# One channel of the z projection moved into the modulation stream

## The chip, the core and the metric

The kernel runs on one NeuronCore of a Trainium2 chip, whose engines work side by side, each through its own queue in order: TensorE (PE in the rows; PEld is its weight loads), VectorE (DVE), ScalarE (ACT), GpSimd (POOL) and SyncE (SP), which here issues most DMAs. The metric is the device time of one execution in microseconds, lower is better.

## The reference, cut to what matters

The block is an RG-LRU and a differential attention side by side, then a mixture of experts, over 1024 tokens of width 1024. The part that the change touches:

```python
mod = jnp.dot(jax.nn.silu(c), w_mod[l]) + b_mod[l]
shift1, scale1, gate1, shift2, scale2, gate2 = jnp.split(mod[:, None, :], 6, axis=-1)
h = rms_norm(x, g_norm1[l]) * (1.0 + scale1) + shift1
proj = jnp.dot(h, w_in[l])
x_lru, z_lru, q, k, v = jnp.split(proj, SPLITS, axis=-1)   # 512 columns each
xc = lax.conv_general_dilated(x_lru, conv_w[l], ...) + conv_b[l]
h_fwd = rg_lru(xc, ..., False)
h_bwd = rg_lru(xc, ..., True)
y_lru = (h_fwd + h_bwd) * jax.nn.gelu(z_lru)
```

After it come the attention on q, k and v, the output product with w_out, the router, and 16 experts.

## The kernel before, in words

h is kept transposed: 8 row blocks of 128 model rows by 1024 tokens. Each product with w_in is done in three parts for exactness: a weight tile is split into a high part (a ScalarE copy) and the low rest (a subtraction on VectorE or GpSimd), h likewise into hh and hl, and wh·hh, wl·hh and wh·hl are summed in PSUM. For one channel block (128 columns of w_in) that is 8 row blocks x 3 parts x 2 halves of 512 tokens = 48 matmuls.

**The modulation stream** (L377 to L440) makes h block by block, in an order written out by hand for TensorE, VectorE and ScalarE (manual_schedule). For row block k: m_load (L281) brings the block's columns of w_mod for shift and scale, m_mm (L293) multiplies part of them by silu(c) on TensorE into tile mp, m_sum (L300) adds the rest on VectorE into acc (L304, L310), m_red (L314) sums acc over partitions on TensorE into the small tile pm, m_col (L319) makes the block's scale and shift columns, h_make (L325) makes hh on ScalarE and hl on GpSimd or VectorE. At once x_mm (L340) multiplies the block with w_in's columns 0 to 255, that is two channel blocks of x_lru (px[0] and px[1]), the wl·hh and wh·hh parts in iteration k and the wh·hl part one iteration later. Iteration k of the loop at L412 works on modulation block k + 2 and on products of block k.

**PSUM** has four tiles of two banks in this phase, two under the tag "pj" and two under "pg". In the stream px[0] and px[1] hold one of each; mp uses the other "pj" and pm the other "pg".

**Behind the stream** the order is found by a planner that lists instructions by priority and modelled time, engine by engine: do_x (L452) is the convolution on VectorE, do_lru (L495) a channel block's gates (products pg on TensorE, tanh and exp on ScalarE tg, tt) and its two scans on VectorE, proj_qk (L576) the dense q and k products (pjq, pjk) with their norms (rq, nq) and a flip to channel order (pbq, pbk; then hq/hk on ScalarE and lq/lk on VectorE), mod_rest (L618) the remaining four modulation rows, 32 loads wr of 512 KB each added up on VectorE into macc, mod_out (L625) their sum over partitions (mq), do_z (L636) one channel block of z (proj_ch, pjz) and fin_lru (L535), which multiplies gelu(z) with the scans' sum. do_z for channels 0 and 1 stands at L657 and L661, behind the k products; their weights are wz0 (L653).

**Buffers that tie the loads to the work:** raw weights go through 5 buffers (rawA), split ones through 6 (strm), the scans through 10 (lru), w0's split parts, macc and the results y_lru share 4 (ylp).

Of the kernel before, what the change touches and what calls it, by code (L numbers as in the profile page):

```python
# [8 lines left out]
F32 = mybir.dt.float32  # L9
F32R = mybir.dt.float32r  # L10
# [8 lines left out]
P = 128  # L19
# [4 lines left out]
NCT = 4  # L24
# [38 lines left out]
KV = (7,)  # L63
KH = (0, 1, 2, 7)
KB = (0, 1, 2, 7)
CAP = 128
RPAD = 56
EPS = 1e-6
# [14 lines left out]
def tile_block(ctx: ExitStack, tc, x, cols, w_mod, b_mod, w_in, wa, wx, lam_qk, relT, w_out, g2, w_router,  # L83
# [5 lines left out]
    def act(out, in_, func=AF.Copy, **kw):  # L89
        return A.activation(out=out, in_=in_, func=func, **kw)  # L90
# [42 lines left out]
    def raw_tile(name, shape):  # L133
        return rawA.tile(shape, F32, tag="raw", bufs=NRA, name=name)
# [4 lines left out]
    def split(src, hi, lo, eng=None):  # L139
        act(hi, src)  # L140
        return (eng or V).tensor_tensor(out=lo, in0=src, in1=hi.bitcast(F32), op=ALU.subtract)  # L141

    def load_half(c0, kk, eng):
        r = raw_tile(f"wi{c0}_{kk}", [P, 4, 256])
        SY.dma_start(out=r, in_=w_in[kk * 512:(kk + 1) * 512, c0:c0 + 256].rearrange("(k p) c -> p k c", p=P))
        hi = strm.tile([P, 4, 256], F32R, tag="s", bufs=NSP, name=f"wi{c0}_{kk}h")
        lo = strm.tile([P, 4, 256], F32R, tag="s", bufs=NSP, name=f"wi{c0}_{kk}l")
        split(r, hi, lo, eng)
        return hi, lo

    def load_in(c0, eng):
        return [load_half(c0, kk, eng) for kk in range(2)]

    phb = ExitStack()
    psb = phb.enter_context(tc.tile_pool(name="psb", bufs=1, space=PSUM, reuse_waits="tile"))
# [125 lines left out]
    def m_load(k):  # L281
        for rh in range(2):
            w = raw_tile(f"wm{k}_{rh}", [P, 4, 2, P]) if rh else v_tile(f"wm{k}_{rh}", [P, 4, 2, P])
            for g in range(2):
                c0 = g * 1024 + k * P
                with tc.issue_after(lds[-1].ins):
                    lds.append(SY.dma_start(out=w[:, :, g, :],
                                            in_=w_mod[rh * 512:(rh + 1) * 512, c0:c0 + P].rearrange("(r p) c -> p r c", p=P)))
            wm[k, rh] = w

    mps, pms = {}, {}

    def m_mm(k):  # L293
        if RP[k]:
            mps[k] = psb.tile([P, 2, P], F32, tag="pj", bufs=2, name=f"mp{k}")
        for r in range(RP[k]):
            g = 32 * (r % 4)
            mm(mps[k][g:g + 32], scz[:, r, :], wm[k, r // 4][:, r % 4], r < 4, r + 4 >= RP[k])
# [13 lines left out]
            V.tensor_tensor(out=part[0], in0=part[0], in1=part[1], op=ALU.add)  # L312

    def m_red(k):  # L314
        pms[k] = psb.tile([P, 2], F32, tag="pg", bufs=2, name=f"pm{k}")
        for g in range(2):
            mm(pms[k][:, g:g + 1], accs[k][:, g, :], ones32[:, 0:1], True, True)

# [21 lines left out]
    def x_mm(k, lo, ms=(0, 1)):  # L340
        for m in ms:
            wh, wl = (w[:, k % 4, m * P:(m + 1) * P] for w in ws0[k // 4])
            for lt, h_ in ((wh, hl[k]),) if lo else ((wh, hh[k]), (wl, hh[k])):
                for n in range(2):
                    mm(px[m][:, n * 512:(n + 1) * 512], lt, h_[:, n * 512:(n + 1) * 512],
                       k == 0 and lt is wh and not lo, k == KT - 1 and lo)

    w0r, wq0 = [], []

    def w0_load(kk):  # L350
# [5 lines left out]
    def w0_split(kk, part):  # L356
        if part == 0:
            ws0.append([ylp.tile([P, 4, 256], F32R, tag="y", bufs=NCT, name=f"w0{c}_{kk}") for c in "hl"])
            act(ws0[kk][0], w0r[kk])
        else:  # L360
            hi, lo = ws0[kk]
            V.tensor_tensor(out=lo, in0=w0r[kk], in1=hi.bitcast(F32), op=ALU.subtract)
# [6 lines left out]
    w0_load(0)  # L369
    for k in range(1, 4):  # L370
        m_load(k)
        if k == KM:
            w0_load(1)
    with tc.issue_after(lds[-1].ins):
# [2 lines left out]
    with tc.manual_schedule(engines={mybir.EngineType.PE, mybir.EngineType.DVE, mybir.EngineType.Activation}):  # L377
        c_silu()
        tables_a()
        act(rst[:, 0:1], epsc, AF.Sqrt)  # L380
        for t in range(NT + 1):
            if t < NT:
                x_stat(t)
            if 1 <= t <= NT:
                if t == NT:
                    m_mm(0)
                    m_sum(0)
                x_flip(t - 1)
                if t == NT:
                    m_red(0)  # L390
            if 2 <= t <= NT:
                x_evac(t - 2)
        w0_split(0, 0)
        m_col(0)
        x_evac(NT - 1, (0,))
        m_mm(1)
        warm(WU1)
        w0_split(0, 1)
        m_sum(1)
        h_make(0)  # L400
        m_red(1)
        m_col(1)
        x_evac(NT - 1, (1,))
        h_make(1)
        x_mm(0, False)
        m_mm(2)
        m_sum(2)
        x_mm(1, False, (0,))
        m_red(2)
        m_col(2)  # L410
        h_make(2)
        for k in range(1, KT + 1):  # L412
            if k + 3 < KT:
                m_load(k + 3)
            if k + 2 < KT:
                m_mm(k + 2)
                m_sum(k + 2)
            if k == KS:
                w0_split(1, 1)
            if k == 1:  # L420
                x_mm(0, True)
            if k == KLT:
                lam_table()
            if k < KT:
                x_mm(k, False, (0, 1) if k > 1 else (1,))
            if 1 < k < KT:
                x_mm(k - 1, True)
            if k + 2 < KT:
                m_red(k + 2)
                m_col(k + 2)  # L430
                i_act, i_pv = h_make(k + 2)
                if k + 2 < KT - 1:
                    i_pool = i_pv
                else:
                    i_dve = i_pv
            if k == KS0:
                w0_split(1, 0)
            if k + 2 in (KW, KW + 1):
                wq0.append(load_half(1024, k + 2 - KW, V))
        x_mm(KT - 1, True)  # L440
    sm1_.close()


# [51 lines left out]
    def do_lru(ct):  # L495
        xc = xc_[ct]
        xh = lt_(f"xch{ct}", None, F32R)
        xl = lt_(f"xcl{ct}", None, F32R)
        split(xc, xh, xl, V if ct in LV else G_)
        hs, st = [], []  # L500
        for d in range(2):
            pre = []
            for gi in range(2):
                pg = psb.tile([P, 1024], F32, tag="pg", bufs=2, name=f"pg{ct}_{d}_{gi}")
                i = d * 4 + ct
                for wi_, (w_, xv) in enumerate(((bdh, xh), (bdl, xh), (bdh, xl))):
                    for n in range(2):
                        mm(pg[:, n * 512:(n + 1) * 512], w_[gi][:, i, :], xv[:, n * 512:(n + 1) * 512], wi_ == 0, wi_ == 2)
                tg = lt_(f"tg{ct}_{d}_{gi}")
                act(tg, pg, AF.Tanh, scale=0.5, bias=hb[:, gi * 8 + i:gi * 8 + i + 1])  # L510
                pre.append(tg)
            ta, ti = pre
            i = d * 4 + ct
            tt = lt_(f"tt{ct}_{d}")
            act(tt, ta, AF.Tanh, scale=nkap[:, i:i + 1], bias=nkap[:, i:i + 1])
            act(ta, ta, AF.Exp, scale=kap[:, i:i + 1], bias=kap[:, i:i + 1])
            sq = lt_(f"sqa{ct}_{d}")
            act(sq, ta, AF.Square)
            V.scalar_tensor_tensor(out=tt, in0=sq, scalar=1.0, in1=tt, op0=ALU.add, op1=ALU.mult)
            V.scalar_tensor_tensor(out=ti, in0=ti, scalar=1.0, in1=xc, op0=ALU.add, op1=ALU.mult)  # L520
            st.append((ta, ti, tt))
        for d in range(2):
            ta, ti, tt = st[d]
            act(tt, tt, AF.Sqrt, scale=0.25)
            G_.tensor_tensor(out=ti, in0=ti, in1=tt, op=ALU.mult)
            if d == 0:
                V.tensor_tensor_scan(out=tt, data0=ta, data1=ti, initial=0.0, op0=ALU.mult, op1=ALU.add)
            else:
                V.tensor_tensor_scan(out=tt[:, ::-1], data0=ta[:, ::-1], data1=ti[:, ::-1], initial=0.0,
                                     op0=ALU.mult, op1=ALU.add)  # L530
            hs.append(tt)
        V.tensor_tensor(out=hs[0], in0=hs[0], in1=hs[1], op=ALU.add)
        hs_[ct] = hs[0]

    def fin_lru(ct, ps):  # L535
        ge = lt_(f"ge{ct}")
# [99 lines left out]
    def do_z(ws, cp, m):  # L636
        fin_lru(2 * cp + m, proj_ch(ws, m, f"pjz{cp}_{m}"))
# [3 lines left out]
    with tc.issue_after(conv.ins):  # L641
        mod_rest(0, 0, 1)
    do_lru(0)
    wq1 = load_in(1280, G_)
    mod_rest(0, 2)
    proj_qk(wk0, 1, 0)
# [3 lines left out]
    proj_qk(wq1, 0, 1)  # L650
    do_lru(1)
    mod_rest(0, 5)
    wz0 = load_in(512, G_)  # L653
    proj_qk(wk1, 1, 1)
    mod_rest(0, 6, 7)
    wx1 = load_in(256, V)
    do_z(wz0, 0, 0)  # L657
    pend.pop()[1]()
    mod_out(0)
    mod_new(1)  # L660
    do_z(wz0, 0, 1)  # L661
    mod_rest(1, 0, 1)
    wr = lru.tile([P, KT, NE], F32, name="wr")
    A.dma_start(out=wr, in_=w_router.rearrange("(k p) e -> p k e", p=P))
# [799 lines left out]
```

## Time and profile before

| | |
|---|---|
| three timed runs | 1180.72, 1180.84, 1183.39 us (median 1180.84) |
| the profiled execution | 1183.49 us, span 1181.8 us |
| busy over the span | PE 1116.1 us (94%), PEld 937.7 (79%), DVE 955.8 (81%), ACT 791.3 (67%), POOL 481.7 (41%) |
| mean granted TensorE clock | 0.977 of full speed |
| chain that ended last | PE 75%, DVE 7%, issue 5%, POOL 5%, DMA 5%, ACT 2% |

Times count from the first instruction of the span. The busy share of a whole kernel mixes stages with different limits, so the stages are read one by one below. "Chain" is the work that ended last, followed back from the end, at each step to what released it.

### The profile page before, as it was taken

What the parts mean: (1) busy time and instruction counts of PE and PEld (TensorE: products, weight loads), DVE (VectorE), ACT (ScalarE), POOL (GpSimd) and SP (SyncE); (2) the same over time, 40 slices, a digit from 0 to 9 for tenths busy, and PEclk for the clock granted to TensorE, in tenths of its full rate; (3) what the DMA queues carried; (4) which work ended last, traced back from release to release, by engine and by line L of the source; (5) the groups of instructions that cost most, each with busy time, mean ns of one, the idle gap of its engine ahead of it and who ended that gap; (6) DMA issues with size and microseconds to landing.
All of it is one profiled execution on the core that took longest, in us unless ns stands there. A gap on an engine that the chain in (4) does not pass through costs nothing.

```text
span 1181.8 us, 17872 instructions
## 1 busy us (share of the span) xinstructions
PE 1116.1 (94%) x6320; PEld 937.7 (79%) x6320; DVE 955.8 (81%) x1242; ACT 791.3 (67%) x1046; POOL 481.7 (41%) x540
## 2 busy tenths in 40 slices
PE   6999899999979999999569999999999999999996
PEld 4698898798869899777447888888888888888885
DVE  6897657875569896543679999999999999999995
ACT  7548282295467787543328887878888787888784
POOL 4693132133086646344534324444323444332400
PEclk9999999999999999999769999999999999999999
DMA  9765625704781505425799999999999999999911
GB/s 334 228 198 177 220 84 170 242 18 112 193 242 45 150 19 180 162 107 211 266 342 330 363 386 380 390 391 402 378 394 393 369 392 410 394 394 386 393 37 18
DMA packets 146994, 304.34 MB, mean 258 GB/s; under 512 B 16973, under 2 KB 43725, under 8 KB 146901
## 3 DMA queue, kind: packets, MB, share of 16 engines
q1 hardware_dynamic: 135008, 279.99, 65.7%
q0 software_dynamic: 5488, 19.45, 6.4%
q10 hardware_dynamic: 6408, 3.77, 1.1%
q8 instruction: 50, 0.82, 0.3%
q14 instruction: 40, 0.32, 0.1%
HBM read 277.95 MB, written 25.21 MB: 257 GB/s over the span
## 4 chain that ended last, share of the span: by engine, by line
PE 75%; DVE 7%; issue 5%; POOL 5%; DMA 5%; ACT 2%; SPq 1%; POOLq 0%; ACTq 0%; DVEq 0%
PE ab L93 28%; PE y L93 13%; PE mix L93 7%; PE pjz L93 4%; PE pjk L93 3%; PE sc L93 3%; PE pjv L93 3%; PE pv L93 3%; PE pw L814 2%; DMA wr<-in_w_mod_dram 2%; POOL wo L886 2%; PE pg L93 1%; DVE macc L623 1%; DMA wo<-in_w_out_dram 1%; PE pf L1348 1%
## 5 line engine op out<-in xcount | busy, mean ns | idle before, releaser
L1248 POOL TENSOR_SCALAR oh<-iot,slot 128x128 bf16<-128x128 bf16 x120 | 146.4, 1234 | 252.5 <-PE pf L1348 252.4
L93 PE MATMUL ab<-wh,xeh 128*128 128x512 f32 x512 | 202.2, 395 | 0.2 <-ACT xeh L90 0.2
L93 PE MATMUL ab<-wh,xel 128*128 128x512 f32 x512 | 199.7, 390 | 0.0
L93 PE MATMUL ab<-wl,xeh 128*128 128x512 f32 x512 | 157.7, 389 | 0.0
L93 PEld LDWEIGHTS ab<-wl,xeh 128*128 128x128 f32 x512 | 96.1, 188 | 20.4
L93 PEld LDWEIGHTS ab<-wh,xel 128*128 128x128 f32 x512 | 96.2, 188 | 19.5 <-DVE xel L1261 0.5
L93 PEld LDWEIGHTS ab<-wh,xeh 128*128 128x128 f32 x512 | 96.1, 188 | 19.5 <-ACT xeh L90 0.5
L141 DVE TENSOR_TENSOR wl<-w_0r,wh 128x1024 fp32r<-128x1024 f32 x79 | 96.8, 1226 | 10.2 <-ACT wh L90 0.4
L90 ACT ACTIVATE wh<-w_0r 128x1024 fp32r<-128x1024 f32 x81 | 86.1, 1062 | 24.8 <-PE ab L93 14.9
L141 DVE TENSOR_TENSOR wl<-w_3r,wh 128x1024 fp32r<-128x1024 f32 x79 | 96.7, 1225 | 6.2
L90 ACT ACTIVATE wh<-w_1r 128x1024 fp32r<-128x1024 f32 x79 | 83.5, 1058 | 23.7 <-PE ab L93 18.9
L90 ACT ACTIVATE wh<-w_3r 128x1024 fp32r<-128x1024 f32 x79 | 83.9, 1062 | 22.0 <-PE ab L93 17.4
L141 DVE TENSOR_TENSOR wl<-w_2r,wh 128x1024 fp32r<-128x1024 f32 x80 | 96.4, 1221 | 2.6 <-ACT wh L90 1.4
L90 ACT ACTIVATE wh<-w_2r 128x1024 fp32r<-128x1024 f32 x80 | 84.7, 1060 | 19.1 <-PE ab L93 18.7
L141 DVE TENSOR_TENSOR wl<-w_1r,wh 128x1024 fp32r<-128x1024 f32 x78 | 92.7, 1220 | 3.9 <-ACT wh L90 2.1
L768 DVE CUSTOM_DVE_ANT_0 p<-sc,bias 128x1024 f32<-128x1024 f32 x64 | 77.7, 1216 | 10.0 <-PE sc L93 9.9
L93 PE MATMUL y<-wh,htl 128*128 128x512 f32 x256 | 82.9, 395 | 0.0
L93 PE MATMUL y<-wh,hth 128*128 128x512 f32 x256 | 80.9, 396 | 0.0
L93 PE MATMUL y<-wl,hth 128*128 128x512 f32 x256 | 79.6, 391 | 0.0
L90 ACT ACTIVATE p<-p,stat 128x1024 f32<-128x1024 f32 x60 | 68.5, 1151 | 9.1 <-DVE stat L768 9.1
L93 PEld LDWEIGHTS pv<-v,wt 128*128 128x128 f32 x512 | 61.7, 192 | 2.5
L93 PE MATMUL pv<-v,wt 128*128 128x128 f32 x512 | 62.1, 275 | 0.0
(459 smaller groups left out, 2862.5 us busy)
## 6 DMA issues: line engine op xcount, KB each, us to landing
w_0r<-in_w_dram SPq DMA_DIRECT2D x81, 512.0 KB, 8.8
w_1r<-in_w_dram SPq DMA_DIRECT2D x79, 512.0 KB, 8.3
w_2r<-in_w_dram SPq DMA_DIRECT2D x78, 512.0 KB, 8.8
w_3r<-in_w_dram SPq DMA_DIRECT2D x77, 512.0 KB, 8.9
wr<-in_w_mod_dram SPq DMA_DIRECT2D x32, 512.0 KB, 4.9
wi<-in_w_in_dram SPq DMA_DIRECT2D x18, 512.0 KB, 4.4
w_5r<-in_w_dram SPq DMA_DIRECT2D x17, 512.0 KB, 8.0
wm<-in_w_mod_dram SPq DMA_DIRECT2D x32, 256.0 KB, 4.8
```

The lines of the kernel that those rows point to most:

```text
L90: return A.activation(out=out, in_=in_, func=func, **kw)
L93: return T.matmul(out, lhsT=lhsT, rhs=rhs, start=start, stop=stop)
L141: return (eng or V).tensor_tensor(out=lo, in0=src, in1=hi.bitcast(F32), op=ALU.subtract)
L623: V.scalar_tensor_tensor(out=macc[i], in0=w, scalar=sc[:, k:k + 1], in1=macc[i], op0=ALU.mult, op1=ALU.add)
L768: V.tensor_tensor_reduce(out=p_, in0=scp[g, j], in1=prs[h][0][:, b0:b0 + S], op0=ALU.add, op1=ALU.min, scale=1.0, scalar=3.0e38, accum_out ...
L814: T.transpose(pw[:, b * P:(b + 1) * P], pt_[g, 0][:, kt * P:(kt + 1) * P], ident)
L886: G_.tensor_tensor(out=r[:, qs], in0=r[:, qs], in1=gate1[:, qs], op=ALU.mult)
L1248: G_.tensor_scalar(out=oh[:, t, :], in0=iot, scalar1=slot[:, e, t:t + 1], scalar2=None, op0=ALU.is_equal)
L1348: T.transpose(pt[:, b * P:(b + 1) * P], sa[:, b * P:(b + 1) * P], ident)
```

## The change

- z_load, z_split and z_mm bring channel block 0 of z (columns 512 to 639) into the stream: one load of 512 KB between those of modulation blocks 2 and 3, the split in iterations 1 (ScalarE) and 2 (VectorE), and from iteration 3 on the six matmuls of row block k - 3. Row blocks 6 and 7 follow behind the last part of x_mm, then the gelu.
- pz takes the "pg" tile that pm had. From block 3 on, mp and pm are parts of one "pj" tile of two banks (mp in the first, pm in the second).
- m_red of a block now stands behind z_mm in its iteration.
- fin_first multiplies the first channel right behind do_lru(0). The place of do_z(wz0, 0, 0) is empty; channel 1's weights come as one column tile (load_col) and its product runs at that place; do_z(wz0, 0, 1) is gone from behind mod_new(1).

```diff
+    def load_col(c0, eng):
+        r = raw_tile(f"wc{c0}", [P, KT, P])
+        SY.dma_start(out=r, in_=w_in[:, c0:c0 + P].rearrange("(k p) c -> p k c", p=P))
+        hi, lo = (strm.tile([P, KT, P], F32R, tag="s", bufs=NSP, name=f"wc{c0}{c}") for c in "hl")
+        split(r, hi, lo, eng)
+        return col_halves(hi, lo)
 
     def m_mm(k):
         if RP[k]:
-            mps[k] = psb.tile([P, 2, P], F32, tag="pj", bufs=2, name=f"mp{k}")
+            if k == 3:
+                mpb.append(psb.tile([P, 8, P], F32, tag="pj", bufs=2, name="mpb"))
+            mps[k] = mpb[0][:, 0:2] if k > 2 else psb.tile([P, 2, P], F32, tag="pj", bufs=2, name=f"mp{k}")
...
     def m_red(k):
-        pms[k] = psb.tile([P, 2], F32, tag="pg", bufs=2, name=f"pm{k}")
+        pms[k] = mpb[0][:, 4, 0:2] if k > 2 else psb.tile([P, 2], F32, tag="pg", bufs=2, name=f"pm{k}")
...
+    wz = [sm1.tile([P, KT, P], F32 if c == "r" else F32R, name=f"wz{c}") for c in "rhl"]
+    def z_load():
+        with tc.issue_after(lds[-1].ins):
+            lds.append(SY.dma_start(out=wz[0], in_=w_in[:, CZ:CZ + P].rearrange("(k p) c -> p k c", p=P)))
+    def z_split(part):
+        if part == 0:
+            act(wz[1], wz[0])
+        else:
+            V.tensor_tensor(out=wz[2], in0=wz[0], in1=wz[1].bitcast(F32), op=ALU.subtract)
+            wzs[:] = col_halves(wz[1], wz[2])
+    def z_mm(k):
+        if not pz:
+            pz.append(psb.tile([P, 1024], F32, tag="pg", bufs=2, name="pz0"))
+        wh, wl = (w[:, k % 4, :] for w in wzs[k // 4])
+        for lt, h_ in ((wh, hh[k]), (wh, hl[k]), (wl, hh[k])):
+            for n in range(2):
+                mm(pz[0][:, n * 512:(n + 1) * 512], lt, h_[:, n * 512:(n + 1) * 512], k == 0 and lt is wh and h_ is hh[k],
+                   k == KT - 1 and lt is wl)
...
     for k in range(1, 4):
         m_load(k)
+        if k == 2:
+            z_load()
...
             if 1 < k < KT:
                 x_mm(k - 1, True)
+            if k > 2:
+                z_mm(k - 3)
             if k + 2 < KT:
                 m_red(k + 2)
...
             if k == KS0:
                 w0_split(1, 0)
+                z_split(0)
+            if k == KS0 + 1:
+                z_split(1)
...
         x_mm(KT - 1, True)
+        z_mm(KT - 2)
+        z_mm(KT - 1)
+        ge0 = ylp.tile([P, S], F32, tag="y", bufs=NCT, name="ylru0")
+        act(ge0, pz[0], AF.Gelu_apprx_tanh)
...
+    def fin_first():
+        V.tensor_tensor(out=ge0, in0=hs_[0], in1=ge0, op=ALU.mult)
+        y_lru.append(ge0)
...
     do_lru(0)
+    fin_first()
...
-    wz0 = load_in(512, G_)
+    wz0 = load_col(CZ + P, G_)
     proj_qk(wk1, 1, 1)
     mod_rest(0, 6, 7)
     wx1 = load_in(256, V)
-    do_z(wz0, 0, 0)
+    fin_lru(1, proj_ch(wz0, 0, "pjz0_1"))
     pend.pop()[1]()
     mod_out(0)
     mod_new(1)
-    do_z(wz0, 0, 1)
```

## Rows read from the trace of the kernel before

**Rows 1.** Busy by stretch: times, length, PE PEld DVE ACT POOL (count), clock, DMA, GB/s.

```profile
23.00:36.50 13.50, 13.46 (x104) 8.91 (x92) 10.21 (x18) 6.88 (x6) 8.71 (x5) 1.00 1.09 331
39.10:59.50 20.40, 20.26 (x104) 15.12 (x105) 17.07 (x28) 12.94 (x12) 12.09 (x13) 0.92 0.60 171
59.50:142.00 82.50, 76.57 (x611) 74.43 (x609) 69.17 (x52) 40.47 (x41) 42.28 (x37) 1.00 0.62 200
142.00:177.10 35.10, 35.08 (x257) 33.86 (x258) 16.32 (x14) 28.56 (x27) 9.76 (x5) 0.95 0.29 100
177.10:188.20 11.10, 11.10 (x53) 9.15 (x52) 7.82 (x6) 3.59 (x5) 3.93 (x2) 1.00 0.29 95
188.20:233.00 44.80, 42.83 (x223) 35.49 (x221) 34.01 (x27) 10.25 (x10) 9.42 (x6) 1.00 0.69 225
```

**Rows 2.** TensorE's waits, 20-60 us (first), 60-150 us: total, times, longest.

```profile
PE pm L93 <- DVE acc L310: 2.7, 1, 2.7
...
PE pg L93 <- ACT tg L90: 2.0, 1, 2.0
PE pbq L593 <- DVE nq L586: 2.0, 1, 2.0
PE pbk L593 <- DVE nk L586: 1.2, 1, 1.2
PE pjq L93 <- POOL wi_1l L141: 0.8, 1, 0.8
```

**Rows 3.** The chain that ended last: start, us, what; block-4 sums, z channels.

```profile
34.11 1.96 DVE acc L310
36.09 2.47 DVE acc L310
...
177.22 10.91 PE pjz L93 x48
...
190.01 11.15 PE pjz L93 x48
```

**Rows 4.** In order of time, the stream: start, us, engine, [idle before <- releaser].

```profile
40.09 1.24 ACT L90 ACTIVATE hh<-xT,shc,acol 128x1024 fp32r<-128x1024 f32 x1 [3.31 <-DVE shc L323]
41.33 1.53 DVE L310 SCALAR_TENSOR_TENSOR acc<-wm,sc,acc 128x256 f32<-128x256 f32 x3
42.68 2.42 POOL L335 TENSOR_TENSOR hl<-xT,hh 128x1024 fp32r<-128x1024 f32 x1 [4.42 <-ACT xT L90]
42.77 3.41 DVE L362 TENSOR_TENSOR w0l<-w,w0h 128x1024 fp32r<-128x1024 f32 x1
44.38 0.65 PEld L93 LDWEIGHTS pm<-ones,acc 128*128 128x128 f32 x4
52.79 0.52 PEld L93 LDWEIGHTS pm<-ones,acc 128*128 128x128 f32 x4 [0.55 <-DVE acc L310]
57.15 1.22 DVE L141 TENSOR_TENSOR wi_0l<-wi,wi_0h 128x1024 fp32r<-128x1024 f32 x1
```

**Rows 5.** The chain again, 90 to 145 us.

```profile
94.44 1.67 PE pg L93 x6
...
129.75 5.32 DMA wr<-in_w_mod_dram
...
141.96 1.97 PE pbq L593 x8
```

**Rows 6.** In order of time, VectorE behind the stream.

```profile
59.54 2.60 DVE L455 TENSOR_SCALAR xc<-pjx,col 128x1024 f32<-128x1024 f32 x2
...
135.16 1.29 DVE L623 SCALAR_TENSOR_TENSOR macc<-wr,sc,macc 128x1024 f32<-128x1024 f32 x1 [4.24 <-DMA wr<-in_w_mod_dram]
```

**Rows 7.** In order of time, TensorE and VectorE, 188 to 233 us.

```profile
188.94 1.06 PE L93 MATMUL mq<-macc,ones 128*32 128x512 f32 x8
...
226.01 2.06 DVE L623 SCALAR_TENSOR_TENSOR macc<-wr,sc,macc 128x1024 f32<-128x1024 f32 x1 [1.64 <-DMA wr<-in_w_mod_dram]
...
232.90 0.73 PE L93 MATMUL pg<-xch,bdh 128*128 128x512 f32 x2 [1.97 <-DVE lk L600]
```

More of the change, by code (lines that the diff above doesn't have):

```diff
@@ L65 @@
 KB = (0, 1, 2, 7)
+CZ = 512
 CAP = 128
@@ L152, in load_in, with col_halves @@
         return [load_half(c0, kk, eng) for kk in range(2)]
+    def col_halves(hi, lo):
+        return [(hi[:, 4 * kk:4 * kk + 4, :], lo[:, 4 * kk:4 * kk + 4, :]) for kk in range(2)]
+    def load_col(c0, eng):
[4 more added lines that the diff above has]
+        return col_halves(hi, lo)
     phb = ExitStack()
@@ L289, in m_load @@
             wm[k, rh] = w
-    mps, pms = {}, {}
+    mps, pms, mpb = {}, {}, []
     def m_mm(k):
         if RP[k]:
-            mps[k] = psb.tile([P, 2, P], F32, tag="pj", bufs=2, name=f"mp{k}")
+            if k == 3:
+                mpb.append(psb.tile([P, 8, P], F32, tag="pj", bufs=2, name="mpb"))
+            mps[k] = mpb[0][:, 0:2] if k > 2 else psb.tile([P, 2, P], F32, tag="pj", bufs=2, name=f"mp{k}")
         for r in range(RP[k]):
@@ L346, in x_mm @@
                        k == 0 and lt is wh and not lo, k == KT - 1 and lo)
+    wz = [sm1.tile([P, KT, P], F32 if c == "r" else F32R, name=f"wz{c}") for c in "rhl"]
+    wzs = []
+    def z_load():
[15 more added lines that the diff above has]
+                   k == KT - 1 and lt is wl)
+    pz = []
     w0r, wq0 = [], []
```

## Prediction

> **What bounds the kernel now.** I read the busy time by stretch first [rows 1], then who waited for whom on TensorE [rows 2], then the chain that ended last [rows 3, 5], and last the instructions in order of time around the change [rows 4, 6, 7]. From 59.5 to 233 us TensorE is the engine that is nearly always busy: 76.57 of 82.50 us, 35.08 of 35.10, 11.10 of 11.10, 42.83 of 44.80 [rows 1]. Its waits there are five: 2.0, 2.0, 1.2 and 0.8 us before 142 us [rows 2], and 1.97 us that end at 232.9 [rows 7]. After the wait that ends at 141.96 us [rows 5] the granted clock drops: 0.95 over the next 35.1 us [rows 1] is a tenth of them at 1.2 GHz instead of 2.4, 3.5 us of which half, 1.7 us, is lost.
>
> The modulation stream is 23 to 59.5 us. The reader should see that its only long hole on TensorE lies at 36.5 to 39.1 us, a wait of 2.7 us for the sums of block 4 [rows 2], and that these sums were not late by their own size: two of them took 1.96 and 2.47 us [rows 3], beside GpSimd's hl subtractions, while three of the same kind took 1.53 us together where GpSimd was quiet [rows 4]. From 39.1 to 59.5 us TensorE is busy 20.26 of 20.40 us [rows 1]. So the stretch into which the change puts its matmuls has next to no hole; the long one lies one iteration before it, between the first two stretches of [rows 1].
>
> **Step 1, the products moved into the stream.** z_mm issues 6 matmuls for each of 8 row blocks, 48. The same 48 take 10.91 us where they stand now [rows 3], 0.227 us each, 1.36 us for six. The first six come in iteration 3, behind the hole. What they can cover is the 0.55 us that the weight load of block 7's sum waits [rows 4]: z_mm(2) stands right ahead of it. End of the stream: 10.9 - 0.55 us later.
>
> **Step 2, the load of the third block.** It is 0.5 MB more on SP, ahead of block 3's modulation weights, while the DMA engines move 331 GB/s and are all busy [rows 1]: 1.5 us later for each load behind it (the weights of blocks 3 to 7, the second half of w0, the row for lambda). Bounds 0 and 1.5 us; I take 0.5, nearer to 0 because TensorE's wait in the stream is for VectorE and none is for a load [rows 2].
>
> **Step 3, the two splits.** z_split(0) is one ScalarE copy of 128x1024, of the size of the 1.24 us one that waits 3.31 us before 40.09 us [rows 4]; it falls into that wait: nothing. z_split(1) is one VectorE subtraction: 1.22 us alone, 3.41 us beside a GpSimd one, as that of w0 [rows 4]. It starts near 40.1 us, and GpSimd is quiet until 42.68 us, so 1.2 us; but it pushes the block-5 sums (done at 41.33 + 1.53 = 42.86 us) by some 0.5 us into the hl subtraction that lasts until 45.1 us. Their weight load on TensorE starts at 44.38 us now [rows 4] and 1.36 us later with z_mm(0) ahead, at 45.7: hidden, barely. If that cover fails it costs up to 2.2 us (3.41 - 1.22). Queued behind on VectorE are w0's second low part and block 5's column; both, too, are wanted 1.36 us later than now.
>
> **Step 4, the sums' tile.** For blocks 3 to 7 product and sum share one PSUM tile, half of it each, and the third block gets the tile that is freed. The instructions are the same; I take 0, and the other end is rival E.
>
> **Step 5, who gets what later.** The convolution of the first two blocks starts when the last low part of x_mm is through. Only 36 of the 48 new matmuls stand ahead of that (8.2 us); z_mm(6) and z_mm(7) come behind. So VectorE's chain (the convolution from 59.54 us [rows 6], then the modulation sums macc) starts 8.2 - 0.55 + 0.5 = 8.1 us later, TensorE's dense projections 10.9 - 0.55 + 0.5 = 10.85 us later. That chain is what TensorE waits for twice, at the gate products of 94.44 us and at the flip of 141.96 us [rows 5]. A lead of 2.75 us for the chain takes away the 2.0 us at 94.4 and 0.75 us of what follows; with it used up, both are level again. Gain 2.75 us; bounds 0 (rival A) and all waits up to 142 us (rival B). The one new VectorE item on this chain is fin_first, about 1.2 us; it stands shortly ahead of a macc that waits 4.24 us for its load [rows 6], and that wait hides it. The early gelu is one more item on ScalarE, which is busy only 40.47 of 82.50 us there [rows 1]: nothing.
>
> **Step 6, what goes.** The first z channel, 10.91 us from 177.22 us [rows 3], where TensorE has no wait: -10.9 us in full, if what follows is ready. With it go one split pair and one buffer pair; the weights of the next x blocks can be split earlier. What follows on VectorE is the second half's modulation sums: they can start after mq at 188.94 us [rows 7], 12 us before the x products at 190.01 + 11.15 = 201.2 us [rows 3]; now mq stands behind the remaining z channel, 1 to 2 us before them. VectorE idles 44.80 - 34.01 = 10.8 us in that stretch [rows 1], part of it for loads (1.64 us at 226.0) [rows 7]. Bounds: -3.7 us (the wait of 1.97 us goes, and a cold clock of 1.7 us as above) and +9.9 us (all that idle time stays, rival C). I take 0: the lk that TensorE waits for comes after loads whose buffers are freed by TensorE's own x products, and these move with it.
>
> **The sum**: 10.9 - 0.55 + 0.5 - 2.75 - 10.9 = -2.8 us; the move itself is worth about nothing, the lead of VectorE's chain is the gain. The profiled execution took 1183.49 us (span 1181.8); with -2.8 that is 1180.7. The three runs have 1180.72, 1180.84 and 1183.39, so the profiled one lies 2.6 us over their median; on the median I predict 1180.84 - 2.8 = 1178.0 us.
>
> **The rivals.**
> A, only moved: the lead is not passed on, since steps of that chain hang on TensorE too (a split waits for the q products to free its buffer). 0 us, 1180.8. For it: steps 1 and 6 cancel, and the stream has no hole. Against: the chain does begin with the convolution.
> B, all waits before 142 us go, 6.0 us [rows 2], and the cold clock behind them, 1.7 us: 1180.8 - 7.7 = 1173.1. For it: VectorE is busy only 69 of 82.5 us there [rows 1], and buffers of the scan come free earlier because channel 0's result is multiplied at once. Against: the chain runs through loads such as that of 5.32 us [rows 5], which a lead does not shorten.
> C, the other side: VectorE becomes late between 188 and 233 us. It has 34.0 - 1.2 = 32.8 us of work left in 44.8 - 11.1 = 33.7 us. If half of its 10.8 us of idle time stays, because its queue is in order and the wr loads come when they come, the gate products now at 232.9 us wait 32.8 + 5.4 - 33.7 = 4.5 us longer, with 1.7 us of cold clock: +6.2 - 2.8 = +3.4, 1184.2; if all stays, 9.9 + 1.7 - 2.8 = +8.8, 1189.6. Middle: 1186. The kernel is slower than before as soon as 3.7 us of that idle time survive.
> D, the stream has room that the busy time of TensorE hides. Weight loads take 15.12 of 20.40 us there, 74%, and 9.15 of 11.10, 82%, in the dense z products [rows 1]: (0.82 - 0.74) / 0.82 of 20.4 is 2.0 us that the new matmuls could fill, 1176.0. Against: the cold clock of that stretch (0.92) and its small sums are in the 74%. The Trainium skill (Perfetto Trace Analysis, Identifying the Most-Contended Engine) says that matmul busy time misjudges how much TensorE has left and that the share of weight loads is the better measure; by that page D would be the likely case, while the row of busy time gives no room.
> E, it does not do what it says: each next product waits until the column of the sum before it is read from the shared tile. The block-4 sum starts at 39.1 us and hh, which needs its column, at 40.09 [rows 2, 4], some 0.4 us after the sum's end; four times that, and once more with w0's subtraction ahead, is about 2.5 us lost: 1180.5.
>
> **How the numbers follow.** Chances: the forecast 0.34 (-1 to -4.5 us; a third of it beyond 0.3%, 3.5 us, about what a measurement of this kernel can tell from no change), A 0.17, B 0.18, C 0.19, D 0.07, E 0.05. Faster by over 0.3%: 0.11 + 0.18 + 0.06 = 0.35. Slower: C, 0.19. Within: the rest, 0.46. The forecast's own range is 1176.3 to 1180; down to B and up to the middle of C, with the bounds of steps 2, 3 and 6, it becomes 1172 to 1187.
>
> **What would show it.** Step 1: a stream that ends 10 to 11 us later, six matmuls of the third block per iteration. Steps 2 and 3: the hole at 36.5 us within 1 us of 2.7, no wait for the block-5 sum. Step 5: no wait for tg near 103 us, that before the flip under 2 us, the convolution from 67 to 68 us. Step 6: at the third channel's gates a wait of at most 2 us; 5 us or more there is C. I am wrong if the stream grows by less than 9 us, or if the part behind 188 us does not come forward with TensorE.

## The result, and the profile after

Four runs of the changed kernel took 1188.54 to 1191.19 us, median 1189.51; four of the kernel before beside them 1180.72 to 1183.39, median 1181.49. The ratio is 1.0067, interval [1.0049, 1.0085]: slower by 7.9 us, where 2.8 us faster was forecast and 1187 was the end of the range. The profiled execution took 1191.19 us (span 1189.3).

Line numbers of the changed kernel lie 1 to 52 higher. First the stretches, columns as in [rows 1], cut where the same work begins and ends:

```profile
39.10:72.10 33.00, 31.78 (x154) 24.96 (x155) 19.66 (x32) 14.32 (x13) 19.61 (x34) 0.95 0.50 155
72.10:157.50 85.40, 77.70 (x608) 75.74 (x608) 67.27 (x50) 41.83 (x42) 34.05 (x16) 0.98 0.58 186
157.50:191.00 33.50, 33.50 (x259) 32.28 (x258) 16.30 (x14) 28.55 (x27) 9.57 (x4) 1.00 0.27 95
191.00:203.90 12.90, 12.90 (x67) 9.95 (x65) 6.86 (x7) 4.48 (x5) 1.07 (x1) 1.00 0.26 83
203.90:238.40 34.50, 30.35 (x165) 26.03 (x161) 29.09 (x23) 7.37 (x8) 8.86 (x7) 1.00 0.75 235
```

The stretch from the end of the stream to the last k products took 82.50 us and takes 85.40; the one behind it 35.10 at a clock of 0.95 and now 33.50 at 1.00. In the traces of e1 to e7, e11, e12 and e15 the same work takes 33.4 to 33.6 us as well (in e3 without its 1.0 us of mq), so I read the 1.6 us as a cold spell of the execution that was profiled before. Of the others only e16's shows it again (35.1 us without mq). Behind 177 us the times of the kernel before are late by that much. From 203.9 to the third channel's gates TensorE idles 4.15 us where it idled 1.97.

Who TensorE waited for, columns as in [rows 2], 20 to 75 and 72 to 330 us:

```profile
PE mpb L94 <- DVE acc L323: 2.1, 1, 2.1
PE mpb L94 <- DVE shc L336: 1.1, 3, 0.4
PE mpb L94 <- DMA wm<-in_w_mod_dram: 0.5, 1, 0.5
...
PE pbk L645 <- DVE nk L638: 4.4, 1, 4.4
PE pg L94 <- DVE lk L652: 4.2, 1, 4.2
PE pg L94 <- ACT tg L91: 3.6, 2, 1.8
PE pbq L645 <- DVE nq L638: 1.0, 1, 1.0
```

Two waits have grown: before the second k flip from 1.2 to 4.4 us, before the third channel's gates from 2.0 to 4.2 us [rows 2, 7]; three for the column (shc) and one for a load of modulation weights (wm) are new in the stream. The chain that ended last, columns as in [rows 3]:

```profile
72.11 1.34 DVE xc L503
...
137.11 1.20 DVE macc L675
138.30 1.14 DVE ylru L584
139.44 1.14 DVE rk L634
...
142.22 1.23 DVE nk L638
...
143.50 1.96 PE pbk L645 x8
...
191.15 10.91 PE pjz L94 x48
...
203.93 16.15 PE pjx L94 x70
...
238.36 2.33 PE pg L94 x6
...
244.37 5.89 DMA wr<-in_w_mod_dram
...
267.55 3.04 PE pg L94 x12
```

Against the trace of before: the convolution begins 9.4 us later (59.54 to 68.93) [rows 6] and its second part, six multiply-adds, 11.3 us (62.05 to 73.38), the x products 2.8 us (201.16 to 203.93) [rows 3], the gates 5.5 us (232.90 to 238.36) [rows 7], the end of the span 7.5 us. A sum and the new multiplication (macc, ylru) stand in the chain right ahead of rk and nk.

In order of time, VectorE, then ScalarE, then GpSimd behind the stream:

```profile
68.93 1.34 DVE L503 TENSOR_SCALAR xc<-pjx,col 128x1024 f32<-128x1024 f32 x1 [5.23 <-PE pjx L94]
72.11 1.34 DVE L503 TENSOR_SCALAR xc<-pjx,col 128x1024 f32<-128x1024 f32 x1 [1.84 <-PE pz L94]
...
80.52 8.76 DVE L675 SCALAR_TENSOR_TENSOR macc<-wr,sc,macc 128x1024 f32<-128x1024 f32 x3
...
72.11 1.03 ACT L91 ACTIVATE ylru<-pz 128x1024 f32<-128x1024 f32 x1 [7.86 <-PE pz L94]
...
81.49 3.36 POOL L142 TENSOR_TENSOR xcl<-xc,xch 128x1024 fp32r<-128x1024 f32 x1
```

The first block's convolution begins at 68.93 us, ahead of the z products' end as forecast; the second waits 1.84 us for the last z product, though it doesn't read it.

### The profile page after: what moved, and what is told of

Read it like the earlier page. It is cut to its first block, busy times and chain, and to the rows that moved or that the text cites. A ratio compares the mean times of both kernels' runs of the same rounds, so it can differ in the third digit from the quotient of the medians.

```text
span 1189.3 us, 17877 instructions
## 1 busy us (share of the span) xinstructions
PE 1117.8 (94%) x6319; PEld 940.3 (79%) x6320; DVE 953.8 (80%) x1243; ACT 792.8 (67%) x1047; POOL 478.7 (40%) x539
## 4 chain that ended last, share of the span: by engine, by line
PE 76%; DVE 8%; DMA 4%; issue 4%; POOL 4%; SPq 2%; ACT 1%; POOLq 0%; DVEq 0%; ACTq 0%
PE ab L94 28%; PE y L94 13%; PE mix L94 7%; PE pjk L94 3%; PE sc L94 3%; PE pv L94 3%; PE pjz L94 3%; PE pjx L94 3%; PE pjv L94 2%; POOL wo L938 2%; DVE macc L675 2%; DMA wr<-in_w_mod_dram 2%; PE pw L866 2%; SPq L298 1%; PE pjq L94 1%
```

## The experiments

Ratios and intervals are against the kernel before on the same chip; us are the ratio times 1181.8. In this measure the change is +7.9 us [5.8, 10.0]. Edits are to the changed kernel unless it says otherwise, and cut to what matters. A difference between two experiments has an interval of 2 to 3 us either way, so small ones are read together with the traces.

**e1, the z weights elsewhere.** The pool of the convolution's tiles opens where that of the stream closes. By the program's map its second tile lies partly over wzl, the low part of the z weights, and so waits for wzl's last reader.

```diff
+    bvec = sm1.tile([NH, 2 * S], F32, name="bvec")
+    wz = [sm1.tile([P, KT, P], F32 if c == "r" else F32R, name=f"wz{c}") for c in "rhl"]
+    xTs.append(sm1.tile([P, KT - KX, S], F32, name="xT1"))
```

> The changed kernel, with the third block's weight tiles at another place in the same pool (behind the first three blocks of x and the bias row), so that neither the second convolution tile nor the two gate-weight tiles lies over them. Theory 1, the overlap cost the lead: the second convolution tile no longer waits for the last z product (1.84 us at 72.11 us), the convolution's second instruction starts near 70.3 instead of 72.1 us, the modulation sums near 77.5 instead of 80.5, the wait before the flip at 143.5 us falls from 4.4 to under 2 us, and the time falls by 2 to 3 us, to 1186.5 to 1187.5. Rival, the chain is held by loads and by TensorE's own products: the convolution starts earlier but the flip's wait stays above 3.5 us and the time stays within 1 us of 1189.5.

1.0061 [1.0047, 1.0075]: +7.2 us, the same within the intervals. VectorE in the trace:

```profile
68.78 2.60 DVE L504 TENSOR_SCALAR xc<-pjx,col 128x1024 f32<-128x1024 f32 x2 [5.16 <-PE pjx L94]
...
78.43 7.96 DVE L676 SCALAR_TENSOR_TENSOR macc<-wr,sc,macc 128x1024 f32<-128x1024 f32 x3
```

The wait is gone and the convolution begins 3.0 us ahead of the q products (71.8), the lead of step 5. But the flip still waits 4.4 us, as the rival had it. The overlap was real, and cost nothing that can be measured.

**e2, the sum ahead of the z products.**

```diff
-            if k > 2:
-                z_mm(k - 3)
             if k + 2 < KT:
                 m_red(k + 2)
                 m_col(k + 2)
+            if k > 2:
+                z_mm(k - 3)
+            if k + 2 < KT:
```

> The changed kernel, with the sum over partitions and the column ahead of the six z products of the iteration instead of behind them, so that the z products stand between the column's read of the shared tile and the next product into it. Theory 2, the shared tile costs the stream: the gap between the sum and the next product (0.99, 0.88, 0.88 us now, 0.43 to 0.54 before) is filled in two of three cases, those waits of 0.38 us go, the stream ends some 0.9 us earlier, and the time falls by about 0.9 us, to 1188.6. Rival, the weight load of the sums now waits longer for VectorE because it stands 1.36 us earlier: a new wait of 0.5 us or more before the sums in each iteration, the stream as long as it was or longer, 1189.5 to 1191.

1.0099 [1.0084, 1.0115]: +11.7 us. TensorE's wait for the sums went from 2.1 us once to 4.1 us in three. The rival held, and more: where the change puts them, the z products do cover the sums.

**e3, the modulation result early.**

```diff
     mod_rest(0, 6, 7)
+    mod_out(0)
+    mod_new(1)
     wx1 = load_in(256, V)
...
-    mod_out(0)
-    mod_new(1)
```

> The changed kernel, with the first half's modulation result (mq) and the start of the second half's sums ahead of the remaining z channel instead of behind it. Theory 3, the late start of the second half's sums costs what is lost behind 188 us: mq comes near 191 instead of 203 us, the first sum of the second half near 195 to 198 instead of 211 us, the wait of 4.2 us for lk at 238 us falls to about 2, and the time falls by 3 to 5 us, to 1184.5 to 1186.5. Rival, the second half's sums are held by their loads and buffers, not by mq: the sums start earlier but end where they did, the wait for lk stays above 3.5 us, and the time stays within 1 us of 1189.5.

1.0080 [1.0065, 1.0095]: +9.5 us, slower than either answer had it. mq came at 191.3 us and the sums from 198.7, but they waited for their loads in front of the convolution of the x products. The wait for lk went, and TensorE's v products waited 4.2 us for that convolution instead:

```profile
219.41 1.28 DVE L675 SCALAR_TENSOR_TENSOR macc<-wr,sc,macc 128x1024 f32<-128x1024 f32 x1 [4.59 <-DMA wr<-in_w_mod_dram]
220.61 1.34 DVE L503 TENSOR_SCALAR xc<-pjx,col 128x1024 f32<-128x1024 f32 x1
```

**e4, the gelu behind.**

```diff
-        act(ge0, pz[0], AF.Gelu_apprx_tanh)
     sm1_.close()
...
+    act(ge0, pz[0], AF.Gelu_apprx_tanh)
     def proj_ch(ws, m, name, tag="pj"):
```

> The changed kernel, with the early gelu behind the loads of the gate weights on ScalarE's queue instead of ahead of them. Theory 4, the gelu at the head of the queue delays these loads: they are issued when their tiles are free, no later than 74.2 us, and the gates come earlier; the gate weights' tiles lie over the z weights too, so alone it gains at most 1 us, 1188.5 to 1189.5. Rival, ScalarE's order costs more than the overlap: the time falls by 2 us or more, below 1187.5.

1.0063 [1.0046, 1.0081], and no test: the planner left the gelu at its place in ScalarE's queue. It is a second measurement of the changed kernel.

**e5, the removal alone; e6, the addition alone.** e5 is the kernel before:

```diff
-    do_z(wz0, 0, 0)
-    pend.pop()[1]()
-    mod_out(0)
-    mod_new(1)
-    do_z(wz0, 0, 1)
+    pz1 = proj_ch(wz0, 1, "pjz0_1")
+    fin_lru(0, pz1)
+    fin_lru(1, pz1)
+    pend.pop()[1]()
+    mod_out(0)
+    mod_new(1)
```

e6 gives the changed kernel that place back as it was before, and takes out the gelu and the early multiplication:

```diff
-        act(ge0, pz[0], AF.Gelu_apprx_tanh)
...
-    fin_first()
...
-    fin_lru(1, proj_ch(wz0, 0, "pjz0_1"))
+    do_z(wz0, 0, 0)
```

> The kernel before, with only the removal: the first z channel's 48 products are left out (both channels' gelu read the second channel's product, so the output is wrong in the first), and the modulation result stands behind the one z channel that is left, as in the changed kernel. The prediction's step 6: the time falls by the whole 10.9 us, to 1170.7. Theory A, VectorE and the loads of the second half's sums keep their own pace: TensorE's x products come 10.9 us earlier, but at 240 us only 6 to 8 us are left and at 310 us 5 to 7 us, so 1174.5 to 1176.5; the wait for lk before the third channel's gates grows from 2.0 to over 3.5 us.

> The changed kernel, with only the addition: the third block's load, splits and 48 products stay in the stream but are not used, and both z channels stand where they stood before; no early gelu, no early multiplication. Theory A: the stream's end costs what it shows, 12.2 us instead of 10.85, and no lead comes back: 1193 to 1194.5; the wait before the k flip, whose queue has no early multiplication and no modulation sums in front of it here, stays near 1.2 us. Rival, the added products cost more than they show in the stream, since the convolution and the gate weights wait for them: above 1195 and a flip's wait over 3 us.

e5: 0.9925 [0.9912, 0.9939], -8.9 us, between the two answers. e6: 1.0109 [1.0094, 1.0125], +12.9 us, with 1.2 us before the flip. So 2.0 us of the removal's 10.9 did not arrive (the wait for lk stayed at 2.1 us, other than I expected; the one for tg behind it grew from 0.5 to 2.7 us, with sums in front of the gates' steps on VectorE), and the addition costs all it adds: no lead came back. Their sum is +4.0; the 3.9 us up to 7.9 arise only when both are there (3.9 give or take some 3 us, by the three intervals).

**e7, the flip's order.**

```diff
+    with tc.issue_after(nks["k0_1"].ins):
+        fin_first()
...
+    with tc.issue_after(nks["k0_1"].ins):
+        mod_rest(0, 6, 7)
```

> The changed kernel, with the early multiplication and the last four sums of the first half queued on VectorE behind the second k norm (nk), as the sums were in the kernel before; nothing else. Theory B, three items of 1.1 to 1.2 us in front of nk cost the flip at 143.5 us: its wait falls from 4.4 to about 1.2 us, and the time by 1.5 to 3 us (the clock falls after the wait behind it as it does in the kernel before, which takes part of it back), to 1186.5 to 1188. Rival, VectorE's chain there hangs on what comes before it: the wait stays above 3.5 us and the time within 1 us of 1189.5.

1.0046 [1.0033, 1.0060]: +5.4 us, 2.5 less. The wait of 4.4 us is gone from TensorE's list, further than theory B had it (1.2), and the time is within its range. VectorE in the trace:

```profile
134.53 1.21 DVE L636 TENSOR_REDUCE rk<-sqk 128x16 f32<-128x1024 f32 x1
136.11 0.25 DVE L638 RECIPROCAL rk<-rk 128x16 f32<-128x16 f32 x1 [0.37 <-ACT rk L91]
136.47 1.23 DVE L640 TENSOR_TENSOR nk<-pjk,rk 128x1024 f32<-128x1024 f32 x1
137.61 1.22 DVE L584 TENSOR_TENSOR ylru<-tt,ylru 128x1024 f32<-128x1024 f32 x1
```

**e8, the second half's sums ahead of the last k products**, with e1's and e7's edits.

```diff
     mod_rest(0, 5)
+    with tc.issue_after(nks["k0_1"].ins):
+        mod_rest(0, 6, 7)
+    mod_out(0)
+    mod_new(1)
+    mod_rest(1, 0)
     wz0 = load_col(CZ + P, G_)
     proj_qk(wk1, 1, 1)
-    mod_rest(0, 6, 7)
+    mod_rest(1, 1)
...
-    mod_out(0)
-    mod_new(1)
-    mod_rest(1, 0, 1)
```

> The changed kernel with three things mended: the weight tiles of the third block away from the convolution's tiles, the flip's order on VectorE as in the run beside it, and the second half of the modulation sums begun ahead of the last k products, in the stretch from 150 to 190 us where VectorE was half idle. Theory A, the second half's sums and their loads did not fit into the shortened stretch: with six to eight of the sixteen taken ahead, the wait for lk before the third channel's gates falls from 4.2 to under 1 us and the time to 1179 to 1183. Rival, the sums fill VectorE's queue in front of the norms of the k products: new waits at the flips between 150 and 200 us, the time above 1185.

1.0057 [1.0043, 1.0071], +6.7 us: the rival. A sum stood in front of the q flip's lq and waited for its load:

```profile
158.66 2.49 DVE L678 SCALAR_TENSOR_TENSOR macc<-wr,sc,macc 128x1024 f32<-128x1024 f32 x1 [4.68 <-DMA wr<-in_w_mod_dram]
161.07 1.27 DVE L655 SCALAR_TENSOR_TENSOR lq<-pbq,gqk,hq 128x1024 fp32r<-128x1024 f32 x1
```

**e9, the z products behind the stream**, with e1's and e7's edits, mp and pm in tiles of their own, the gelu held behind the gate weights, and another order on GpSimd.

```diff
-            if k > 2:
-                z_mm(k - 3)
...
-        z_mm(KT - 2)
-        z_mm(KT - 1)
+        for k in range(KT):
+            z_mm(k)
```

> The changed kernel with all 48 z products behind the last x product (none in the stream), the sums in tiles of their own as before, the z weights away from the convolution's tiles, the gelu behind the gate weights on ScalarE, the starting memsets of the sums ahead of the gate weights' low parts on GpSimd, and the flip's order on VectorE as in e7. The convolution then starts at 60 us while TensorE's q products start at 71: a full lead of 10.9 us. Theory of the lead (step 5 as forecast, only that the change gave none): the waits before the flips of 6 us in all shrink to 2 or less, and the time is 1181 to 1184, 3 to 6 us under e7's 1186.9. Rival, the lead is worth nothing because the chain hangs on the loads wr and on TensorE's own q and k products: the waits for tg, nq and nk stay above 4 us in sum, and the time is 1185.5 or more.

1.0023 [1.0011, 1.0035]: +2.7 us, between the two; so are the waits before the flips, 2.8 us for 6.0 before. With so many edits at once the 2.7 us less than e7 can't be put down to the lead. The convolution ran from 60.69 us, 11.5 us ahead of the q products (72.2), but the planner queued the sums behind the first q norm, and most of the lead lay idle:

```profile
63.20 7.22 DVE L500 SCALAR_TENSOR_TENSOR xc<-pjx,col,xc 128x1022 f32<-128x1022 f32 x6
84.91 1.22 DVE L636 TENSOR_REDUCE rq<-sqq 128x16 f32<-128x1024 f32 x1 [14.48 <-ACT sqq L91]
```

**e10, six sums fewer**, on e7.

```diff
-    mod_rest(1, 2, 3)
+    mod_rest(1, 2)
...
-    mod_rest(1, 4)
...
-    mod_rest(1, 5, 6)
+    mod_rest(1, 6)
```

> The kernel of e7 with six of the sixteen sums of the second half and their loads left out (rows 3, 4 and 5 of the modulation weights, so the output is wrong). Theory A, behind 200 us the chain is bound by the backlog of these sums on VectorE and their loads: the wait for lk before the third channel's gates falls from 4.2 to 2.0 us or less, the waits for tg behind it go, and the time falls by 3 to 4.5 us against e7, to 1182.5 to 1184. Rival, the wait for lk comes from the order around the flip and not from the backlog: it stays above 3.5 us and the time falls by less than 1.5 us, to 1185.5 or more.

0.9997 [0.9981, 1.0013]: 5.8 us under e7, more than theory A asked for; the wait for lk is gone from TensorE's list, that for tg behind it stays (1.7 us). The part behind 200 us is bound by these sums and loads; which of the two binds it e10, which leaves out both, can't tell.

**e11, the shared tile alone; e12, the load and the splits alone.** e11 is the kernel before with the m_mm and m_red of the change; e12 is e6 without its products and with the sums in their own tiles:

```diff
-            if k > 2:
-                z_mm(k - 3)
...
-        z_mm(KT - 2)
-        z_mm(KT - 1)
```

> The kernel before, with product and sum of blocks 3 to 7 in one PSUM tile as in the changed kernel, and nothing else. Rival E of the prediction: each next product waits for the column's read, four gaps grow by 0.4 to 0.55 us, the stream ends 1.3 to 2.2 us later and the time is 1182.8 to 1184. The prediction's step 4: nothing, 1181.5.

> The kernel before, with only the load of the third block's weights and its two splits in the stream (no product, sums in tiles of their own, both z channels where they were, their weights loaded as before). Steps 2 and 3 of the prediction: 0.5 us for the load, nothing for the splits: 1182. Theory A, the stream ran 1.3 us longer than its products and the shared tile alone explains that: 1181.5 to 1182.2. Rival, the load and the splits cost what add-only showed over 10.9: 1183.3 or more, with a longer wait for a load or for block 5's sum.

e12: 1.0003 [0.9991, 1.0014], +0.4 us [-1.1, 1.7]: step 2's 0.5. In its trace a product waits 1.5 us for a load (wm), the sums of block 4 are waited for 1.6 us instead of 2.7, and the q products begin 1.3 us later than before. e11: 1.0055 [1.0035, 1.0074], far over both, but its 12 times fall into two groups, five from 1182.0 to 1184.5 and seven from 1188.4 to 1194.2. Its profile is of the first group (1182.01); there the q products begin 2.5 us later than before, and one of the waits for the column is:

```profile
51.89 0.64 PE L93 MATMUL mpb<-wm,scz 128*32 128x256 f32 x8 [1.70 <-DVE shc L325]
```

The column stands behind a small table operation that took 2.33 us on VectorE, and the next product behind the column. In the change the same operation takes 2.37 us, but six z products stand ahead of the sum there, and the wait is 0.4 us.

**e13, lk first; e14, lk first and the result early**, both on e9. The diff is e13's; e14 has e3's edit too.

```diff
-    mod_rest(1, 4)
...
-    mod_rest(1, 5, 6)
+    with tc.issue_after(lks["k1_0"].ins):
+        mod_rest(1, 4)
+        mod_rest(1, 5, 6)
```

> The kernel of e9 with the sums of rows 4 to 7 of the second half queued on VectorE behind the k flip's low part (lk) that the third channel's gates wait for; nothing left out. Theory A, the backlog: the wait of 4.2 us there falls to 2.0 us, as it was before, but the eight sums come behind it among the gates and most of it is lost again: 1182.5 to 1184. Rival, the order alone was the cause of what e10 took away: 1179 to 1181.

> The kernel of e13 with the first half's modulation result ahead of the remaining z channel too, so that six of the second half's sums are in VectorE's queue ahead of the x products' convolution and none between the convolution and lk. Theory A: fewer sums are left behind 230 us, the wait for lk is 2.0 us or less and the time is 1180 to 1182.5, level with or under the kernel before (1181.5 to 1182). Rival, loads: the sums ahead of the convolution wait for their loads there (4.6 us in e3) and hold up the flip of the last k block: 1183.5 or more.

e13: 1.0017 [1.0003, 1.0030]; e14: 0.9995 [0.9986, 1.0004]. Both as theory A had them: the order takes the wait for lk away (the one for tg behind it grows from 1.1 us in e9 to 3.4 in e13 and 2.4 in e14), but the time comes only when the sums start earlier too.

**e15, e11 once more.** No edit.

> The kernel of e11 once more, to see in the profile of another execution where its times, 1182 to 1194, spread. If it comes out above 1187: the waits of TensorE for the column (0.38, 0.79 and 1.70 us in e11's profile) or the sums beside GpSimd's subtractions are longer and the stream ends 3 us or more later than 62 us; or the stream ends at 62 us and the loss lies behind it, with the granted clock below 0.95 in some stretch.

1190.79 us. Stretches of this execution, columns as in [rows 1], cut where the same work begins and ends, within 0.4 us:

```profile
39.00:64.10 25.10, 22.00 (x105) 16.50 (x106) 17.08 (x29) 13.02 (x12) 14.37 (x16) 0.86 0.53 148
64.10:87.50 23.40, 20.33 (x170) 20.13 (x168) 23.30 (x17) 5.62 (x6) 16.68 (x27) 1.00 0.50 148
87.50:114.00 26.50, 24.75 (x156) 23.27 (x157) 21.05 (x15) 21.09 (x20) 7.32 (x3) 0.87 0.71 236
```

and of e11's own:

```profile
39.00:62.20 23.20, 20.34 (x105) 15.74 (x106) 17.64 (x29) 13.03 (x12) 12.79 (x16) 0.93 0.54 160
62.20:82.30 20.10, 20.10 (x169) 20.10 (x168) 19.57 (x18) 5.57 (x6) 18.44 (x27) 1.00 0.64 196
82.30:106.00 23.70, 21.95 (x161) 20.57 (x160) 19.52 (x13) 19.86 (x19) 8.04 (x4) 1.00 0.66 224
```

The same program: 1.9 us more in the stream, 3.3 in the q products, which had to wait, and 2.8 behind them, with the clock lower in the first and the last. The waits for the column are the same in both (3.2 us in four), and the stream ends at 64 us, not 3 us or more behind 62; so of the two answers that I expected the lower clock is the better one, and it is not the whole: 3.1 of the 3.3 us are one wait for a q norm (nq). What decides between the groups stays open.

**e16, e14's mends on the kernel before; e17, the same on the change with its products in the stream.** Diff of e16 against before; e17 has it with e1's and e7's edits:

```diff
+    mod_out(0)
+    mod_new(1)
     wx1 = load_in(256, V)
...
-    mod_out(0)
-    mod_new(1)
...
-    mod_rest(1, 4)
...
-    mod_rest(1, 5, 6)
+    with tc.issue_after(lks["k1_0"].ins):
+        mod_rest(1, 4)
+        mod_rest(1, 5, 6)
```

> The kernel before, z channel and stream untouched, with the two edits to the second half's sums that e14 has: the modulation result ahead of the first z channel, rows 4 to 7 of the sums behind lk on VectorE. If these two edits help by themselves: 1177.5 to 1180, and e14's tie with the kernel before is theirs, not the moved product's. If they only mend what the shortened stretch broke (theory A): the kernel before has no backlog there (wait for lk 2.0 us), so 1180.5 to 1183.

> The changed kernel with its products left in the stream and the sums in the shared tile, and the mends of e14 behind it: weight tiles elsewhere, flip's order, modulation result ahead of the z channel, rows 4 to 7 behind lk. Theory: behind 90 us it is e14; what is left is the place of the 48 products, in the stream without a lead or behind it with one. With e9 against e7 (2.7 us) that is 1183 to 1185. Rival, the lead matters only while the flip's order is bad: then it equals e14, 1180.5 to 1182.

e16: 1.0008 [0.9993, 1.0023]; the mends show no gain without the change. e17: 1.0005 [0.9992, 1.0018], +0.6 us: 4.8 under e7, 7.3 under the change, and level with the kernel before. The interval overlaps e14's, so whether the products stand in the stream or behind it can't be told here. TensorE's waits in e17, 60 to 330 us:

```profile
PE pg L94 <- ACT tg L91: 4.3, 2, 2.5
PE pbk L648 <- DVE nk L641: 1.2, 1, 1.2
PE pbq L648 <- DVE nq L641: 1.0, 1, 1.0
...
```

Neither 4.4 nor 4.2 is left; of the waits for tg the second, at 258 us, is 2.5 us where it was 0.5 before. No version is shown to be faster than the kernel before: e14's interval ends above 1.

## Why the prediction was wrong

**Where the 7.9 us are.** By edits that bring them back: 2.5 us in VectorE's order before the k flip (e7); 4.8 us in the second half's sums behind 188 us (e17 against e7, with the weight tiles moved, which alone changed nothing that can be measured); 0.6 us remain. Each is a difference with 2 to 3 us of interval either way, but the traces place them alike. From the first q product to the first x product, with the same products in each, it is 131.9 us in the change (131.6 to 131.9 in e2 to e4), 130.5 in e1, 127.6 in e7 and 127.0 in e17, against 127.8 in e5, where the stream is the old one. From the first x product to an attention product (sc) that waits 6.9 us in all of them it is 152.0 us before, 154.4 in e5, 155.7 in the change, 155.8 in e7 and 150.8 in e17. The first and the last of these stretches end with these products:

```profile
353.03 1.22 PE L93 MATMUL sc<-kh,qs 128*128 128x512 f32 x2 [6.91 <-DVE stat L768]
350.24 1.22 PE L94 MATMUL sc<-kh,qs 128*128 128x512 f32 x2 [6.95 <-DVE stat L826]
```

By the forecast's own terms, 10.7 us were missed: 4.8 in the addition and its lead (12.9 for 8.1), 2.0 in the removal (-8.9 for -10.9), 3.9 in the two together.

**Steps 1 to 3** held. The q products begin at 71.91 instead of 59.72 us, 12.2 us later; 10.85 of that was forecast. No sum of block 5 was waited for, the hole at 36.5 us was 2.1 us, the load costs 0.4 in time (e12). The reason given for step 2, that TensorE waits for no load in the stream, did not hold: every trace with this load in the stream has a wait for wm of 0.3 to 1.5 us, and none without it has one. The wait for the sums is shorter by part of that, and so the 0.5 came out in part by luck.

**Step 4** ("I take 0") failed: 0.99, 0.88 and 0.88 us lie between a sum and the next product where 0.54, 0.43 and 0.43 lay, from start to start, 1.35 us more in all. That is as much as the 12.2 lacks, though smaller terms cancel in it: six products take 1.40 us instead of 1.36, and the hole before them is shorter. Rival E was the right mechanism; its wait stands in the profile (shc, 1.1 us in three). It is no large part of the 7.9 us: e17 has the same shared tile and the same 1.1 us of wait. The change with separate tiles and its products in the stream was not run.

**Step 5** is the step that failed first: "the convolution starts ... 8.1 us later" and "gain 2.75 us". In the change the convolution began 9.4 us later, and its second part 11.3 us, because of a buffer that I didn't look up; TensorE was 12.2 us later, so that the lead was 0.9 us. e1 gave 2.9 us of lead and nothing came of it, but it still had the bad order before the k flip. e17 has the same lead with the order mended, and from the q to the x products it takes 127.0 us for the 127.8 of e5, which has none: 0.8 us of the 2.75 at most. So rival A's reason is the better one: the chain hangs on more than its start. What ate the lead can be read, though no run tested it alone. From the convolution's second part to the first q norm (nq) VectorE takes 15.4 us before the change and 18.7 in e1. The first three sums were, before the change:

```profile
69.19 3.67 DVE L623 SCALAR_TENSOR_TENSOR macc<-wr,sc,macc 128x1024 f32<-128x1024 f32 x3
```

They now take 8.76 us (7.96 in e1), beside GpSimd's low parts of the convolution and the gate weights. These began, before the change and in it, at:

```profile
73.61 2.40 POOL L141 TENSOR_TENSOR bdl<-bd,bdh 128x1024 fp32r<-128x1024 f32 x1
79.10 2.41 POOL L142 TENSOR_TENSOR bdl<-bd,bdh 128x1024 fp32r<-128x1024 f32 x1 [3.01 <-ACT bdh L91]
```

That is 11.6 us behind the convolution's second part before, and 5.7 us in the change. Before, GpSimd was busy with a small table until 73.5 us, and the low parts fell on later sums; in the change the table is done at 69.0 us, and they begin as soon as the gate weights are there. The early gelu ahead of the gate weights' loads on ScalarE is not the cause: in e6, which has no gelu there, it is 4.7 us. The Trainium skill (SBUF — State Buffer, Terms) says that VectorE and GpSimd lock a shared pair of ports against each other for a whole instruction; these rows agree, as both sides take longer: GpSimd's xcl beside the sums 3.36 us, its bdl ahead of them 2.41.

**The cover of fin_first** ("that wait hides it") failed too. The planner made the order anew, and the multiplication and three sums came to stand just ahead of the steps to the two k norms; each takes 1.1 to 1.3 us. e7, which moves the multiplication and the sums at once, shows the price, 2.5 us.

**Step 6** ("I take 0" for what follows the removal) was wrong by 2.0 us alone (e5) and by 4.8 in the full change (e17 against e7), where the result of the first half comes at 202.9 us, 1 us ahead of the x products instead of 12, as the step had seen itself. Its reason for 0, that the loads ahead of lk move with TensorE's x products, held for lk in e5 (2.1 us) and not for the sums behind it. Rival C named this mechanism, VectorE late with the second half's sums, and e10 shows it; even its worst case, 1189.6, is the time that came, but by chance: it let 11.6 us stay behind 188 us and kept the lead of 2.75, while 4.8 us are what came back there.

**Rivals B and D** were wrong: the waits up to the q flip grew from 6.0 to 7.6 us (4.4 for nk, 1.7 for tg, 1.0 for nq, 0.5 for the low parts), and weight loads fill 24.96 of 33.00 us of the stream, 76%, hardly more than the 74% of before; the measure by weight loads had found room that the stream did not have.

The chances were ill set as well: 0.19 for slower, all on one place, while three places could lose 2 us or more each.

## What to carry to other kernels

Moving work out of a stretch of TensorE took, here, its cover from whatever VectorE and the loads did beside it: add up what is left there, and begin it earlier in the same edit. When a planner orders the queues, a new instruction off the path can change what stands in front of one on it, so compare each engine's order ahead of every wait, and look up what the new tiles lie over. Undo one half of a move at a time: add alone and remove alone showed in two runs that some 3.9 of the 10.7 us belonged to neither.

## What the runs showed of the hardware

The granted clock is not the same from one execution of a program to the next. In the q products' stretch e11 and e15 both have 1.00; in the stream they have 0.93 and 0.86, and in the stretch behind the q products 1.00 and 0.87, where 0.87 means that about a quarter of it went by at 1.2 instead of 2.4 GHz. In e15's stream pairs of 128x512 products took 1.05 instead of 0.62 us behind TensorE's waits of 2.2 us (near 39 us) and of 1.72 us (near 52 us); in e11 they did so behind the first alone, and behind its wait of 1.70 us at 51.89 us they took 0.63. The same program came out between 1182.0 and 1194.2 us. A profile of one execution can thus hold a spell that the median has not, as the 1.6 us before 177 us in the profile of the kernel before.
